# Gate and up projections in Strassen's products in every group from the third on, and two groups ahead of the first down part

## Chip, core and metric

The kernel runs on one core of a Trainium2 chip. The metric is the device time of one execution in microseconds (us). A run gives one such time; beside the runs there is one profiled execution, whose trace gives the start and duration of the instructions on each engine: PE (TensorE, matmuls), PEld (its weight loads), DVE (VectorE), ACT (ScalarE), POOL (GpSimd) and SP (which only issues transfers here).

## What is computed

A decoder trunk of two layers on x of 1 × 512 × 1024 in float32. Each layer has a mixer and then a gated ConvFFN, both behind an RMS norm and with a residual:

```python
def gated_conv_ffn(x, w_gate, w_up, conv_w, conv_b, w_down):
    g = jnp.einsum('bsd,df->bsf', x, w_gate)
    g = causal_dwconv3(g, conv_w) + conv_b
    up = jnp.einsum('bsd,df->bsf', x, w_up)
    return jnp.einsum('bsf,fd->bsd', jax.nn.silu(g) * up, w_down)
...
    hn = rms_norm(h, norm_ffn[layer])
    h = h + gated_conv_ffn(hn, w_gate[layer], w_up[layer], conv_ffn[layer],
                           b_conv_ffn[layer], w_down[layer])
```

The hidden width is 2816, that is 22 tiles of 128 columns. The mixers and the final norm are not touched by the change.

## The kernel before

**Precision.** Every float32 operand is split into a high and a low half of a reduced format (whi/wlo for weights, a_hi/a_lo for activations, hgh/hgl for the normalized input), and a product is three matmuls: high × high, high × low, low × high (`mm3`, lines L133 to L135). A weight is split by ACT (high half, L128) and DVE (low half, L129), or, with `summed`, by ACT twice and an accumulating transfer that POOL issues (L120 to L122); an activation is split by `split` (ACT L247, DVE L249).

**Groups and parts.** The hidden width is worked through in groups of two tiles: group f holds tiles f and f+1, f = 0, 2, ... 20. For each group, gate and up are multiplied, the gate goes through the width-3 convolution (`conv`, ACT L504 and DVE L506) and silu (L512), is multiplied by up, and the result is split into the group's activations a_f and a_f+1. The down projection is done in parts, each over the tiles of one or two groups: in layer 0 `project` (its PSUM tiles are named d; DVE adds them to h at L292), in layer 1 a loop in `ffn1` (PSUM tiles dn; DVE adds to y at L1009). `PARTS` says which tiles each part covers. Each part comes after its groups:

```python
    PARTS = ((0, 2), (2, 6), (6, 10), (10, 14), (14, 18), (18, 22))
    BOTH = (6, 10, 14, 18)
```

so the order before is group 0, down part of tiles 0 and 1, groups 2 and 4, down part of tiles 2 to 5, groups 6 and 8, and so on.

**Four ways to multiply a group** (`hidden`). Group 0 (`direct`, not normalized) multiplies the input as it stands ahead of the norm, 96 matmuls of 512 columns, and the factor of the norm is applied afterwards by DVE (L555) and POOL (L558); while it runs, `normalize` prepares the normalized input (x by DVE at L571, its halves at L575 and L576) and the sums of its blocks (L583 to L586) that the block products need. Group 2 (`direct`, normalized) does the same 96 matmuls on the normalized input. Groups 4, 8, 12, 16 and 20 (`seven`) compute up in Strassen's seven block products and gate as 48 matmuls of 512 columns. Groups 6, 10, 14 and 18 (`both`) compute gate and up each in seven block products. A block product (`multiply`, L623) is 12 matmuls of 256 columns; one seventh less work than the direct form. It needs sums of blocks of the weights, made by DVE into `sum` tiles and split, and the products are put together in `kept` and in the padded rows by ACT copies from PSUM (`both`: L681; `seven`: L765) and DVE adds (`both`: L686). In a group, several products share a PSUM bank (`BANK`): 1, 6, 7 and 4 use bank "a", one after the other.

**Buffers.** Raw weights have 4 buffers, split weights 6 each of high and low, `sum` tiles 3, `kept` 1, activations a 4, convolution tiles c 2, silu tiles s 3, padded rows 3, PSUM 7 banks and one auxiliary. The queues of each engine run in the order that a scheduler writes at build time from the program order and its own estimates; SP issues the loads of raw weights (`fetch`, L110).

Of the kernel before, what the change touches and what calls it, by code (L numbers as in the profile page):

```python
# [8 lines left out]
F32 = mybir.dt.float32  # L9
# [3 lines left out]
ALU = mybir.AluOpType  # L13
PSUM = bass.MemoryType.PSUM

P = 128
# [14 lines left out]
def tile_trunk(ctx: ExitStack, tc: tile.TileContext, x, norm_mix, norm_ffn, final_norm,  # L31
# [3 lines left out]
    nc = tc.nc  # L35
# [9 lines left out]
    def mm_bank(name):  # L45
        return ps_mm.tile([P, 512], F32, tag="mm", name=name)
# [69 lines left out]
    def summed(raw, a, b, name):  # L116

        hi = wp.tile([P, a, b], F32R, tag="whi", bufs=6, name=f"whi_{name}")
        lo = wp.tile([P, a, b], F32R, tag="wlo", bufs=6, name=f"wlo_{name}")
        nc.scalar.activation(lo, raw, AF.Copy, scale=-1.0)  # L120
        nc.gpsimd.dma_start(lo, raw, accum_op=ALU.add)  # L121
        nc.scalar.activation(hi, raw, AF.Copy)  # L122
        return hi, lo

    def parts(raw, a, b, name):
        hi = wp.tile([P, a, b], F32R, tag="whi", bufs=6, name=f"whi_{name}")
        lo = wp.tile([P, a, b], F32R, tag="wlo", bufs=6, name=f"wlo_{name}")
        nc.scalar.activation(hi, raw, AF.Copy)  # L128
        nc.vector.tensor_tensor(lo, raw, hi.bitcast(F32), ALU.subtract)  # L129
        return hi, lo  # L130

    def mm3(ps, lhs, rhs, start, stop):
        nc.tensor.matmul(ps, lhs[0], rhs[0], start=start, stop=False)  # L133
        nc.tensor.matmul(ps, lhs[0], rhs[1], start=False, stop=False)  # L134
        nc.tensor.matmul(ps, lhs[1], rhs[0], start=False, stop=stop)  # L135
# [27 lines left out]
    def hg_k(k):  # L163
        return hg[k][0], hg[k][1]
# [104 lines left out]
    def padded_tile():  # L269
        turn[0] += 1  # L270
        return padded[turn[0] % NPADDED]
# [199 lines left out]
            return nxt  # L471


    PARTS = ((0, 2), (2, 6), (6, 10), (10, 14), (14, 18), (18, 22))
    HALF = S // 2
    BOTH = (6, 10, 14, 18)
    NP = NK // 2
    PAIRS = [k for i in range(NP) for k in (i, i + NP)]

    def ffn_weights(layer, f, order):  # L480
        cs = slice(f * P, (f + 2) * P)
        return {(key, half): fetch(
            (w_ffn_gate if key == "g" else w_ffn_up)[layer][half * 512 : (half + 1) * 512, cs]
            .rearrange("(k p) c -> p k c", p=P), 4, 256, f"{key}{layer}_{f}_{half}")
            for key, half in order}

    class Ffn:
# [143 lines left out]
        def halves(self, hi, lo, src):  # L631
            nc.scalar.activation(hi, src, AF.Copy)
            nc.vector.tensor_tensor(lo, src, hi.bitcast(F32), ALU.subtract)
# [72 lines left out]
            nc.vector.tensor_tensor(s0, kept[:, :2, :], s0, ALU.mult)  # L706
            self.act(f, s[0])

        def seven(self, f):
            layer, ap, n = self.layer, self.ap, f"{self.layer}_{f}"  # L710
            raws = ffn_weights(layer, f, [(key, half) for key in "ug" for half in range(2)])
            r0, r1 = raws["u", 0][0], raws["u", 1][0]
            stat = {}

            def pair(name):
                return self.unit(f"{name}_{n}")

            halves = self.halves

            def put(product, hi_lo, i):  # L720
                stat[product] = hi_lo[0][:, i], hi_lo[1][:, i]

            w = pair("a11")
            halves(w[0][:, 0], w[1][:, 0], r0[:, :, :P])
            put(1, w, 0)
            gate = [parts(*raws["g", 0])]
            s23 = ap.tile([P, 2, 4, P], F32, tag="sum", bufs=3, name=f"s23_{n}")
            s14 = ap.tile([P, 2, 4, P], F32, tag="sum", bufs=3, name=f"s14_{n}")
            nc.vector.tensor_tensor(s14[:, 0], r0[:, :, P:], r1[:, :, P:], ALU.add)
            nc.vector.tensor_tensor(s23[:, 0], s14[:, 0], r0[:, :, :P], ALU.subtract)  # L730
            nc.vector.tensor_tensor(s23[:, 1], r0[:, :, :P], r0[:, :, P:], ALU.subtract)
            w = pair("s23")
            halves(*w, s23)
            put(6, w, 0)
            put(7, w, 1)
            gate.append(parts(*raws["g", 1]))
            nc.vector.tensor_tensor(s14[:, 1], r1[:, :, :P], s23[:, 0], ALU.subtract)
            w = pair("s14")
            halves(*w, s14)
            put(5, w, 0)  # L740
            put(3, w, 1)
            hi, lo = summed(*raws["u", 1])
            for i, product in enumerate((2, 4)):
                c = slice(i * P, (i + 1) * P)
                stat[product] = hi[:, :, c], lo[:, :, c]

            banks = {}

            def multiply(product):
                return self.multiply(banks, f"u{n}", product, stat[product])  # L750

            def gates(half):
                for k in PAIRS[half * 4 : half * 4 + 4]:
                    for j in range(2):
                        if j not in banks:
                            banks[j] = mm_bank(f"g{j}{n}")
                        hi, lo = gate[k // 4]
                        c = slice(j * P, (j + 1) * P)
                        mm3(banks[j], (hi[:, k % 4, c], lo[:, k % 4, c]), hg_k(k),
                            k == PAIRS[0], k == PAIRS[-1])  # L760

            kept = ap.tile([P, 3, HALF], F32, tag="kept", bufs=1, name=f"kept{n}")

            def keep(i, ps):
                nc.scalar.copy(kept[:, i, :], ps)  # L765

            def add(i, ps):
                nc.vector.tensor_tensor(kept[:, i, :], ps, kept[:, i, :], ALU.add)

            keep(0, multiply(1))  # L770
            gates(0)
            keep(1, multiply(6))
            gates(1)
            c, s = [], []
            for j in range(2):
                t = padded_tile()
                nc.scalar.copy(t[:, 2:], banks[j])
                c.append(self.conv(t, f + j))
            keep(2, multiply(7))
            for j in range(2):  # L780
                s.append(self.silu(c[j], f + j))
            ps = multiply(5)
            p2 = multiply(2)
            add(2, ps)
            add(0, p2)
            ps = multiply(4)
            nc.vector.tensor_tensor(s[1][:, HALF:], kept[:, 2, :], s[1][:, HALF:], ALU.mult)
            nc.vector.tensor_tensor(s[1][:, :HALF], ps, s[1][:, :HALF], ALU.mult)
            self.act(f + 1, s[1])
            add(1, multiply(3))  # L790
            s0 = s[0].rearrange("p (a b) -> p a b", a=2)
            nc.vector.tensor_tensor(s0, kept[:, :2, :], s0, ALU.mult)  # L792
            self.act(f, s[0])

        def hidden(self, f, before=lambda i, j: None):
            if f == 0:
                def first(i, j):
                    before(i, j)
                    if (i, j) == (1, 0):
                        self.norm.rstd_tokens()  # L800
                    elif (i, j) == (2, 2):
                        self.r = self.norm.rstd_spread()

                ch = self.pair_weights(0, [("g", 0), ("u", 0), ("g", 1), ("u", 1)])
                rest = self.direct(0, False, (range(4),), ch, first)
                self.ch = self.pair_weights(2, [("g", 0), ("g", 1), ("u", 0), ("u", 1)], "g")
                for kp in range(NP):
                    self.normalize(kp)
                rest()
            elif f == 2:  # L810
                self.direct(2, True, ((0, 1), (2, 3)), self.ch)()
            elif f in BOTH:
                self.both(f)
            else:
                self.seven(f)

    def ffn0(norm):
        nonlocal prm1
        with tc.tile_pool(name="f0", bufs=1) as ap:
            def sums(kp):  # L820
                return [ap.tile([P, 2, HALF], F32R, name=f"t23{i}_{kp}") for i in "hl"]

            ffn = Ffn(0, prm0, norm, ap, sums)
            nxt = None
            for a, b in PARTS:
                for f in range(a, b, 2):
                    ffn.hidden(f)
                if b == NF:
                    prm1 = params1()
                    nxt = Norm("m1", lambda k: prm1("mix", k))  # L830
                project(f"d0_{a}", w_ffn_down[0], ffn.acts, list(range(a, b)), nxt)
            return nxt
# [126 lines left out]
    def ffn1(norm):  # L959
        with tc.tile_pool(name="f1", bufs=1) as ap:  # L960
# [17 lines left out]
                if i < 2:  # L978
                    turn_residual(j, i)

            for a, b in PARTS:
                for f in range(a, b, 2):
                    ffn.hidden(f, before=before)
                last = b == NF
                if last:
# [60 lines left out]
    n = mixer0()  # L1046
    n = ffn0(n)
# [32 lines left out]
```

## Time and profile before

| | |
|---|---|
| runs | 1043.4, 1040.25, 1040.7 us (median 1040.7) |
| profiled execution | 1041.7 us, of which the span (first to last instruction) is 1040.0 us |
| mean granted TensorE clock | 0.983 |
| PE busy | 999.5 us, 96% of the span |
| PEld busy | 865.6 us, 83% |
| DVE busy | 660.4 us, 64% |
| ACT busy | 495.0 us, 48% |
| POOL busy | 91.9 us, 9% |

A row of a group of waits names the engine, tile and line that waited, what released it, and the total, the count and the longest in us. A row of single instructions has its start, its duration, engine, line, operation, written tile and read tiles, then shape, and in brackets the idle time of the engine ahead of it with what ended it. A row of a stretch has the window, its length, the busy time of each engine with its instructions, the granted clock as a share of full speed, the share of the DMA engines' time and GB/s.

### The profile page before, as it was taken

How to read it: one execution, taken by the hardware profiler on the slowest of the kernel's cores; microseconds unless marked ns; L12 is line 12 of the kernel's file. 1: busy time of each engine (PE TensorE's matmuls, PEld its weight loads, DVE VectorE, ACT ScalarE, POOL GpSimd, SP SyncE). 2: the span in 40 equal slices, each digit the busy share in tenths (PEclk: the TensorE clock that was granted, in tenths of full speed). 3: DMA queues.
4: the chain of work that ended last, by engine and by line, in shares of the span. 5: the costliest groups of instructions: out<-in, count | busy, mean ns of one | idle time of the engine just before them, and what ended most of it. 6: DMA issues, size and time to landing. Idle time of an engine off the chain costs nothing.

```text
span 1040.0 us, 13829 instructions
## 1 busy us (share of the span) xinstructions
PE 999.5 (96%) x5475; PEld 865.6 (83%) x5475; DVE 660.4 (64%) x977; ACT 495.0 (48%) x725; POOL 91.9 (9%) x107
## 2 busy tenths in 40 slices
PE   8999996899999999999999999949999999999997
PEld 6888885688988989899888888837889899898985
DVE  5976539638576586756833545495477756767576
ACT  6423447235453536436655434662426436353463
POOL 3041121100000000000300001220000000000000
PEclk9999998799999999999999999979999999999999
DMA  7432244324354453554343223451335544354432
GB/s 234 166 102 81 83 120 110 94 77 123 104 142 112 133 138 106 142 135 124 119 130 101 81 86 97 101 117 45 89 94 142 142 124 141 82 142 142 123 82 81
DMA packets 80462, 119.25 MB, mean 115 GB/s; under 512 B 4133, under 2 KB 53517, under 8 KB 80397
## 3 DMA queue, kind: packets, MB, share of 16 engines
q1 hardware_dynamic: 73580, 98.96, 30.2%
q0 software_dynamic: 5472, 17.83, 9.7%
q10 hardware_dynamic: 1344, 1.58, 0.5%
q8 instruction: 43, 0.70, 0.3%
q14 instruction: 23, 0.18, 0.1%
HBM read 98.42 MB, written 2.10 MB: 97 GB/s over the span
## 4 chain that ended last, share of the span: by engine, by line
PE 91%; DVE 3%; issue 3%; DMA 2%; ACT 0%; SPq 0%; POOL 0%; DVEq 0%; POOLq 0%; ACTq 0%
PE d L133 4%; PE d L134 4%; PE dn L135 4%; PE dn L133 4%; PE dn L134 4%; PE d L135 4%; PE g L133 4%; PE g L134 4%; PE g L135 3%; PE gu L133 2%; PE gu L135 2%; PE gu L134 2%; PE v L133 1%; PE oo L135 1%; PE u L134 1%
## 5 line engine op out<-in xcount | busy, mean ns | idle before, releaser
L133 PE MATMUL dn<-whi_dn,a_hi 128*128 128x512 f32 x176 | 69.3, 395 | 14.9 <-ACT a_hi L247 14.9
L133 PE MATMUL d<-a_hi,whi_d 128*128 128x512 f32 x176 | 68.1, 398 | 14.6 <-ACT a_hi L247 14.6
L134 PE MATMUL d<-a_lo,whi_d 128*128 128x512 f32 x176 | 69.4, 396 | 0.0
L134 PE MATMUL dn<-wlo_dn,a_hi 128*128 128x512 f32 x176 | 68.9, 393 | 0.0
L135 PE MATMUL d<-a_hi,wlo_d 128*128 128x512 f32 x176 | 68.9, 392 | 0.0
L135 PE MATMUL dn<-whi_dn,a_lo 128*128 128x512 f32 x176 | 68.5, 394 | 0.0
L506 DVE SCALAR_TENSOR_TENSOR c<-rows,prm,c 128x512 f32<-128x512 f32 x88 | 66.5, 770 | 0.4
L133 PE MATMUL g<-hgh,whi_g 128*128 128x512 f32 x160 | 62.5, 391 | 0.0
L134 PE MATMUL g<-hgl,whi_g 128*128 128x512 f32 x160 | 62.5, 391 | 0.0
L135 PE MATMUL g<-hgh,wlo_g 128*128 128x512 f32 x160 | 62.2, 389 | 0.0
L1009 DVE TENSOR_TENSOR y<-dn,y 128x512 f32<-128x512 f32 x48 | 32.8, 690 | 37.1 <-PE dn L135 37.0
L133 PEld LDWEIGHTS dn<-whi_dn,a_hi 128*128 128x128 f32 x176 | 33.4, 190 | 22.7 <-ACT a_hi L247 16.0
L133 PEld LDWEIGHTS d<-a_hi,whi_d 128*128 128x128 f32 x176 | 33.3, 191 | 22.6 <-ACT a_hi L247 15.9
L129 DVE TENSOR_TENSOR wlo_dn<-raw_dn,whi_dn 128x1024 fp32r<-128x1024 f32 x22 | 26.8, 1224 | 35.4 <-ACT whi_dn L128 35.4
L129 DVE TENSOR_TENSOR wlo_d<-raw_d,whi_d 128x1024 fp32r<-128x1024 f32 x22 | 26.8, 1224 | 35.4 <-ACT whi_d L128 35.4
L129 DVE TENSOR_TENSOR wlo_g<-raw_g,whi_g 128x1024 fp32r<-128x1024 f32 x24 | 29.3, 1222 | 30.4 <-ACT whi_g L128 26.6
L292 DVE TENSOR_TENSOR h<-d,h 128x512 f32<-128x512 f32 x48 | 32.7, 689 | 20.1 <-PE d L135 19.5
L247 ACT ACTIVATE a_hi<-s 128x512 fp32r<-128x512 f32 x44 | 27.4, 628 | 34.3 <-DVE s L792 13.3
L121 POOL DMA_DIRECT2D wlo_u<-raw_u x18 | 15.4, 858 | 306.6 <-ACT wlo_u L120 175.6
L129 DVE TENSOR_TENSOR wlo_u<-raw_u,whi_u 128x1024 fp32r<-128x1024 f32 x16 | 19.6, 1224 | 34.2 <-ACT whi_u L128 34.1
L135 PEld LDWEIGHTS dn<-whi_dn,a_lo 128*128 128x128 f32 x176 | 33.3, 189 | 8.5 <-DVE a_lo L249 1.3
L134 PEld LDWEIGHTS d<-a_lo,whi_d 128*128 128x128 f32 x176 | 33.6, 191 | 7.9 <-DVE a_lo L249 0.7
(911 smaller groups left out, 3135.7 us busy)
## 6 DMA issues: line engine op xcount, KB each, us to landing
raw_u<-in_w_ffn_up_dram SPq DMA_DIRECT2D x36, 512.0 KB, 3.8
raw_g<-in_w_ffn_gate_dram SPq DMA_DIRECT2D x36, 512.0 KB, 4.5
raw_d<-in_w_ffn_down_dram SPq DMA_DIRECT2D x22, 512.0 KB, 3.6
raw_dn<-in_w_ffn_down_dram SPq DMA_DIRECT2D x22, 512.0 KB, 3.7
wlo_u<-raw_u POOLq DMA_DIRECT2D x18, 512.0 KB, 5.2
wlo_g<-raw_g POOLq DMA_DIRECT2D x12, 512.0 KB, 5.1
raw_oe<-in_w_out_even_dram SPq DMA_DIRECT2D x8, 512.0 KB, 3.5
raw_g<-in_w_ffn_gate_dram SPq DMA_DIRECT2D x16, 256.0 KB, 2.8
```

The costliest lines, as they stand in the source:

```text
L121: nc.gpsimd.dma_start(lo, raw, accum_op=ALU.add)
L129: nc.vector.tensor_tensor(lo, raw, hi.bitcast(F32), ALU.subtract)
L133: nc.tensor.matmul(ps, lhs[0], rhs[0], start=start, stop=False)
L134: nc.tensor.matmul(ps, lhs[0], rhs[1], start=False, stop=False)
L135: nc.tensor.matmul(ps, lhs[1], rhs[0], start=False, stop=stop)
L247: nc.scalar.activation(hi, src, AF.Copy, scale=scale)
L292: nc.vector.tensor_tensor(h[k], ps, h[k], ALU.add)
L506: nc.vector.scalar_tensor_tensor(c, t[:, i : S + i], prm("cf", i * NF + ft), c, op0=ALU.mult, op1=ALU.add)
L1009: nc.vector.tensor_tensor(dst, ps, dst, ALU.add)
```

## The change

`PARTS` gets a first entry that says which groups are multiplied ahead of each part. Groups 0 and 2 now both come ahead of the first down part (tiles 0 and 1); group 4 alone stands ahead of the second, which still covers tiles 2 to 5. Every group from 4 on is multiplied by `both`; `seven` and `BOTH` are gone. For each layer five groups thus change from `seven` to `both`, ten in all.

```diff
-    PARTS = ((0, 2), (2, 6), (6, 10), (10, 14), (14, 18), (18, 22))
+
+    PARTS = (((0, 2), 0, 2), ((4,), 2, 6), ((6, 8), 6, 10), ((10, 12), 10, 14),
+             ((14, 16), 14, 18), ((18, 20), 18, 22))
     HALF = S // 2
-    BOTH = (6, 10, 14, 18)
...
-        def seven(self, f):
...
             elif f == 2:
                 self.direct(2, True, ((0, 1), (2, 3)), self.ch)()
-            elif f in BOTH:
+            else:
                 self.both(f)
-            else:
-                self.seven(f)
...
-            for a, b in PARTS:
-                for f in range(a, b, 2):
+            for groups, a, b in PARTS:
+                for f in groups:
                     ffn.hidden(f)
...
-            for a, b in PARTS:
-                for f in range(a, b, 2):
+            for groups, a, b in PARTS:
+                for f in groups:
                     ffn.hidden(f, before=before)
```

The order of products in `both`, the banks they use and the pairs of groups that a down part covers from tile 6 on are as before. Groups 6 and 8, 10 and 12, 14 and 16, 18 and 20 stand next to each other as before, but now both of each pair are `both`; group 4, which followed group 2, now follows the first down part.

More of the change, by code (lines that the diff above doesn't have):

```diff
@@ L707, in both @@
             self.act(f, s[0])
-        def seven(self, f):
[L710 to L793, printed above, removed]
```

## Prediction

> **What bounds the kernel now.** I read the page first, then the PE waits, then stretches of the span by stage, then the rows of single instructions around the two longest waits.
>
> ```profile
> PE 999.5 (96%) x5475; PEld 865.6 (83%) x5475; DVE 660.4 (64%) x977; ACT 495.0 (48%) x725; POOL 91.9 (9%) x107
> PE 91%; DVE 3%; issue 3%; DMA 2%; ACT 0%; SPq 0%; POOL 0%; DVEq 0%; POOLq 0%; ACTq 0%
> PE dn L133 <- ACT a_hi L247: 14.9, 2, 14.3
> PE d L133 <- ACT a_hi L247: 14.6, 2, 14.2
> ```
>
> TensorE is busy for 999.5 of 1040.0 us and holds 91% of the chain that ended last; VectorE has 64%, ScalarE 48%. So time goes only where PE idles or where PE gets fewer or faster matmuls. Two waits stand out (us in total, times, longest): the first part of each layer's down projection (d in layer 0, dn in layer 1) waits for the activation of group 0. The change touches both sources, the idle and the amount of matmul work.
>
> The stretches, as window, length, then busy time and count of PE, PEld, DVE, ACT, POOL, the granted clock, the DMA share and GB/s:
>
> ```profile
> 172.25:186.71 14.46, 0.26 (x2) 0.00 (x0) 14.46 (x25) 10.74 (x18) 5.33 (x5) 0.62 0.62 125
> 186.71:201.10 14.39, 13.95 (x48) 10.43 (x49) 10.16 (x15) 1.96 (x3) 1.50 (x1) 0.79 0.17 56
> 201.10:222.90 21.80, 21.80 (x98) 18.06 (x97) 8.81 (x10) 7.88 (x11) 0.00 (x0) 1.00 0.15 49
> 265.84:286.00 20.16, 20.16 (x170) 20.16 (x170) 11.24 (x17) 10.73 (x17) 0.86 (x1) 1.00 0.38 105
> 286.00:307.00 21.00, 21.00 (x133) 19.09 (x133) 14.51 (x22) 13.83 (x22) 0.86 (x1) 1.00 0.56 151
> 307.00:328.84 21.84, 21.84 (x98) 18.00 (x98) 16.52 (x26) 6.58 (x8) 0.85 (x1) 1.00 0.47 121
> ...
> 686.92:701.38 14.46, 0.16 (x1) 0.00 (x0) 14.46 (x25) 10.73 (x18) 5.28 (x5) 0.64 0.62 121
> 701.38:715.23 13.85, 13.27 (x48) 9.72 (x49) 9.56 (x13) 1.76 (x3) 1.50 (x1) 0.88 0.08 26
> 780.00:800.30 20.30, 20.30 (x170) 20.18 (x170) 13.26 (x19) 12.26 (x19) 0.85 (x1) 1.00 0.59 157
> 800.30:821.30 21.00, 21.00 (x133) 19.08 (x133) 14.51 (x22) 13.83 (x22) 0.85 (x1) 1.00 0.56 151
> ```
>
> In order: the idle after group 0, the first down part, group 2 (96 matmuls of 512 columns), group 6 (both gate and up in block products), group 8 (only up in block products), a down part; then the same idle and first down part in layer 1, and its groups 6 and 8. Outside the first-part stretches PE has no idle at all.
>
> **First part: two groups ahead of it.** Today PE waits for a_0 and a_1 with DVE busy through all 14.46 us: it normalizes the input of group 2 while it also owes the gating of group 0. Afterwards PE runs on a lowered clock:
>
> ```profile
> 186.71 1.22 PE L133 MATMUL d<-a_hi,whi_d 128*128 128x512 f32 x2 [14.20 <-ACT a_hi L247]
> 188.93 0.63 PE L134 MATMUL d<-a_lo,whi_d 128*128 128x512 f32 x1
> 190.85 1.22 PE L133 MATMUL d<-a_hi,whi_d 128*128 128x512 f32 x2 [0.44 <-ACT a_hi L247]
> 194.30 0.39 PE L133 MATMUL d<-a_hi,whi_d 128*128 128x512 f32 x1
> 705.53 0.50 PE L133 MATMUL dn<-whi_dn,a_hi 128*128 128x512 f32 x1 [0.58 <-ACT a_hi L247]
> ```
>
> At full clock a 512-column matmul costs 21.80 / 96 = 0.227 us, so the 48 of the first part cost 10.9. From the end of group 0 to the end of its down part it takes 14.46 + 14.39 = 28.85 us in layer 0 and 14.46 + 13.85 = 28.31 in layer 1. If group 2 covers the wait completely, 28.85 − 10.9 − 0.26 (the small transpose in the idle stays) = 17.7 and 28.31 − 10.9 = 17.4 us go: together 35.1. Of that 6.4 us are not idle but matmuls on a lowered clock and the second wait (14.39 and 13.85 against 10.9).
>
> The Trainium skill ("TensorE: Matmul & The Clock Gate", the table of what matters for kernels and Part 1) says that an idle gap beyond some 3 us drops the array to half rate and about 3.4 us of activity restore it. That would be a loss of about 1.7 us per restart, an estimate from that page, and a gain of about 32 in place of 35.1; the trace agrees on the direction, but the stretches measure 3.5 and 2.95 us, and I use those.
>
> Is group 2 ready to run at 172.25? It needs the normalized input in pairs (0 and 4, 1 and 5, 2 and 6, 3 and 7), each pair feeding 2 × 6 matmuls = 2.73 us of its gate half, so the last is wanted at 172.25 + 8.2 = 180.4. DVE today:
>
> ```profile
> 172.76 0.70 DVE L576 TENSOR_TENSOR hgl<-x,hgh 128x512 fp32r<-128x512 f32 x1
> 176.96 1.30 DVE L576 TENSOR_TENSOR hgl<-x,hgh 128x512 fp32r<-128x512 f32 x2
> 190.17 0.63 ACT L247 ACTIVATE a_hi<-s 128x512 fp32r<-128x512 f32 x1 [2.76 <-DVE s L561]
> 190.84 0.68 DVE L249 TENSOR_TENSOR a_lo<-s,a_hi 128x512 fp32r<-128x512 f32 x1
> 691.63 1.29 DVE L576 TENSOR_TENSOR hgl<-x,hgh 128x512 fp32r<-128x512 f32 x2
> 704.85 0.63 ACT L247 ACTIVATE a_hi<-s 128x512 fp32r<-128x512 f32 x1 [2.76 <-DVE s L561]
> 182.05 1.50 SPq L110 DMA_DIRECT2D raw_g<-in_w_ffn_gate_dram  x2
> ```
>
> Pair 2/6 is done at 173.46, wanted at 177.7; pair 3/7 at 178.26, wanted at 180.4. In layer 1, 692.92 against 686.92 + 8.2 = 695.1. No wait, with about 2 us in hand. Group 2 then ends at 172.25 + 0.26 + 21.8 = 194.3, and the last operand of group 0 lands at 191.5 today; group 2's own copies and convolutions now stand in the same DVE and ACT queues and push it by an estimated 0.5 us. Cover: 2.3 us; were it gone, each us of lateness costs one us per layer. In layer 1, 686.92 + 21.8 = 708.7 against 705.5, 3.2 us. PSUM has seven banks; group 0 holds four and group 2 opens two at once and two 10.9 us later, by when group 0's two gate banks have been read. Group 4 begins at 205.3 instead of 222.9; its second pair of raw weights is issued at 182.05 and its splits fall into the first down part, where DVE is busy 10 of 14 us and ACT 2. That I cost at nothing; its first products are the ones with the earliest weights.
>
> **Groups 4, 8, 12, 16, 20: gate in block products too.** Each swaps 48 matmuls of 512 columns for 84 of 256. From the rows: 168 matmuls in 20.16 us are 0.120 each; the mixed group is 84 × 0.120 + 48 × 0.227 = 21.0, as measured. Saved per group: 21.00 − 20.16 = 0.84 in layer 0, 21.00 − 20.30 = 0.70 in layer 1, for ten groups 4.2 + 3.5 = 7.7 us.
>
> A rule of the skill speaks against this: "Larger matmuls are more efficient than smaller matmuls, when possible" ("Perfetto Trace Analysis", section on matmuls), and the clock-gate page (back-to-back issue gap) gives 81 ns at 128 columns and 131 at 512 with weight loads in the stream. Interpolated, an estimate from that page, a 256-column one is 0.75 of a 512-column one and the swap would lose 1.9 us per group. The row above disagrees: 0.120 against 0.227 is 0.53. What the row does concede is PEld at 20.16 of 20.16: weight loads have no slack left in such a group.
>
> Added work off PE per group, by code: on DVE four more sums and one more split of 512 columns (as the a_lo row above, 0.68) and three adds from PSUM, 5 × 0.68 + 3 × 0.42 = 4.7 us:
>
> ```profile
> 287.28 0.42 DVE L686 TENSOR_TENSOR kept<-u_6e,kept 128x256 f32<-128x256 f32 x1
> ```
>
> On ACT the splits come to some 2.5 wide copies more, 2.6 us by the wlo_u row below (1.05), and POOL issues one more summed weight. A part of two groups and a down part becomes 2 × 20.2 + 21.8 = 62.2 us of PE against 11.24 + 14.51 + 16.52 + 4.7 = 47 us of DVE. Throughput holds; order decides.
>
> **Two such groups in a row** (8 pairs: 6-8, 10-12, 14-16, 18-20 in each layer) are new, and no row shows them. Today ACT behind group 6:
>
> ```profile
> 285.47 0.71 ACT L504 ACTIVATE c<-rows,prm 128x512 f32<-128x512 f32 x1
> 286.08 0.71 ACT L512 ACTIVATE s<-c,prm 128x512 f32<-128x512 f32 x1
> ...
> 288.59 0.71 ACT L512 ACTIVATE s<-c,prm 128x512 f32<-128x512 f32 x1
> 289.20 0.61 ACT L247 ACTIVATE a_hi<-s 128x512 fp32r<-128x512 f32 x1
> 289.73 1.05 ACT L120 ACTIVATE wlo_u<-raw_u 128x1024 fp32r<-128x1024 f32 x1
> 291.45 0.63 ACT L247 ACTIVATE a_hi<-s 128x512 fp32r<-128x512 f32 x1 [0.68 <-DVE s L706]
> 291.99 0.35 ACT L765 COPY kept<-u_8a 128x256 f32<-128x256 f32 x1
> ...
> wlo_u<-raw_u POOLq DMA_DIRECT2D x18, 512.0 KB, 5.2
> ```
>
> The convolution, silu and split of the old group keep ACT until 291.99, 6.0 us after the new group began, and only then is its first product copied out of PSUM. Today that copy is needed at 7 us (12 block matmuls and 24 wide ones come first: 1.44 + 5.47). In the changed kernel the gate's product 6 follows in the same bank and, in program order, would start after three products, at 4.3 us. The built order moves other products ahead of it, 55 matmuls in all, so it starts at 55 × 0.120 = 6.6. My queue of ACT work puts the copy's end at 6.4 to 6.7, more splits standing ahead of it than today. Two more near ties: the second summed weight of up, issued near 6.5 and 5.2 us under way, lands at 11.7 where it is wanted at 11.5 to 11.9; and the down part after the pair wants a_8 at 24 × 0.227 = 5.4 us, where the tail above gives 291.45 + 0.63 − 286.00 = 6.1 for the same operand with other splits in its way, about 5 without them. Bounds for each pair: nothing, if the ties fall well; 2.4 us (6.7 − 4.3), if the reordering buys nothing; less than nothing is excluded, since PE's matmul count is fixed. I take 0.5, because the nearest row with such a group on a full engine queue (layer 1, 20.30 against 20.16) lost 0.14, and there are three ties: 8 × 0.5 = 4 us.
>
> **Sum.** −35.1 − 7.7 + 4.0 = −38.8 us. The profiled execution took 1041.7, so 1002.9; it lies 1.0 above the median of 1040.7, so the forecast is 1002. With no stall and both layers at 0.84 it would be 1040.7 − 35.1 − 8.4 = 997. A difference of 0.3% (3 us, the spread of the three runs) is what a measurement here can tell from none.
>
> **Rivals.**
> 1. *The pairs stall.* ACT's backlog delays the first copy by the full 2.4 us in every pair. Eight pairs lose 19 instead of 4: 1017. For: ACT's rows above are back to back. Against: the built order was made around that wait.
> 2. *The idle moves.* Group 2 or group 4 runs into unfinished normalization, late a_1 or late splits, 5 us per layer: 1012. For: DVE is busy in every microsecond of the old idle, and the cover is only 2 us. Against: the rows already have all normalized pairs before they would be wanted.
> 3. *Slower.* DVE and ACT fall behind for good inside each pair: each of the copies and PSUM adds waits behind the splits of the next part, banks stay held, and raw weight buffers come free late. It decides once a pair loses more than (35.1 + 7.7) / 8 = 5.4 us; at 6 us each, 48 − 42.8 = +5, 1046. Against: 47 us of DVE in 62.
> 4. *Weight loads bind.* PEld is at 100% in such groups; if each product cost 3.4 us more per group (0.75 of a wide matmul, 0.170 × 168 − 0.170 × 84 − 48 × 0.227 = 3.4), ten groups add 34 and the result is about 1040.7 − 35.1 + 34 + 4 = 1044. The skill's figures above point there, both measured stretches against it.
>
> That the change does nothing can't be: the built order has group 2 ahead of the first down matmul in both layers and 84 products in all ten groups.
>
> **Chances.** Forecast, 994 to 1010: 0.73. Rival 1: 0.12. Rival 2: 0.09. Rival 3: 0.04. Rival 4: 0.01; another 0.01 for no change. The range 995 to 1014 takes the forecast case, rival 2 and some of rival 1. Faster 0.94, same 0.01, slower 0.05.
>
> **What would show it.** Right: no PE wait on a_hi L247 above 1 us; the granted clock at 1.00 after group 0 and 0.99 or more overall; PE's count 5475 + 10 × 36 = 5835, its busy time near 986 (999.5 − 7.7 − the 5.4 that the first parts' matmuls are busy beyond 10.9); group 4 starting about 17.5 us earlier; 20.2 us for groups 4 to 20. Wrong: PE waits on ACT copies (L681) or DVE adds (L686) of some 2 us, eight times; a wait on hgl or on summed weights at the head of group 2 or 4; stretches of block products above 21 us.

## The result and the profile after

The changed kernel took 1006.16 us (median of four runs, 1005.03 to 1007.18) against 1041.34 (four runs, 1040.25 to 1043.4): a ratio of 0.966, 95% interval 0.9639 to 0.9681, or 35 us less. Its profiled execution took 1007.18 us, with a span of 1005.5 and a mean granted clock of 0.996.

The page and PE's waits of the changed kernel (engine, tile and line that waited, what released it, total, times, longest):

```profile
PE 988.0 (98%) x5835; PEld 875.6 (87%) x5835; DVE 699.3 (70%) x1057; ACT 521.9 (52%) x775; POOL 100.8 (10%) x117
PE 81%; issue 7%; DMA 5%; DVE 5%; ACT 2%; POOL 0%; SPq 0%; ACTq 0%; DVEq 0%; POOLq 0%
PE g_18e L624 <- DVE rows L692: 3.0, 2, 2.4
PE xt_ps L357 <- DMA xt<-in_x_dram: 2.4, 1, 2.4
PE g_6e L624 <- DVE rows L692: 1.1, 1, 1.1
PE u_10a L624 <- ACT kept L682: 1.0, 1, 1.0
PE g_10e L624 <- DVE rows L692: 0.3, 1, 0.3
```

Both 14 us waits on a_hi are gone. PE has 360 matmuls more, as counted, and is busy 11.5 us less. New are five small waits in groups of block products: four on DVE's add to the gate's rows (L692, L691 before) and one on an ACT copy. DMA has come up from 2% to 5% of the chain that ended last, DVE from 3% to 5%, issue from 3% to 7%.

The stretches of the changed kernel, columns as before: group 2 and then the first down part in layer 0, group 4, group 8; group 18 in layer 0; and in layer 1 groups 6, 8, 18 (a down part stands between 8 and the next).

```profile
173.58:195.35 21.77, 21.77 (x98) 18.02 (x96) 21.77 (x35) 16.70 (x27) 6.82 (x6) 1.00 0.47 97
195.35:206.23 10.88, 10.88 (x50) 9.01 (x49) 10.88 (x17) 5.68 (x7) 0.88 (x1) 1.00 0.46 112
206.23:226.38 20.15, 20.15 (x170) 20.15 (x168) 11.82 (x17) 11.40 (x19) 0.86 (x1) 1.00 0.56 153
268.35:288.58 20.23, 20.23 (x171) 20.23 (x169) 14.75 (x23) 14.39 (x24) 0.86 (x1) 1.00 0.59 158
434.89:455.88 20.99, 20.40 (x170) 20.20 (x168) 14.34 (x23) 12.13 (x19) 1.72 (x2) 1.00 0.43 114
742.67:764.32 21.65, 20.58 (x170) 20.25 (x168) 15.41 (x24) 13.70 (x21) 1.86 (x3) 1.00 0.63 155
764.32:784.48 20.16, 20.16 (x171) 20.16 (x169) 14.03 (x21) 13.75 (x23) 0.86 (x1) 1.00 0.61 154
932.80:955.82 23.02, 20.58 (x169) 20.25 (x168) 14.81 (x23) 13.22 (x21) 1.87 (x3) 1.00 0.62 137
```

The first down part takes 10.88 us at clock 1.00, with DVE just as busy as in the old idle: its work now lies under PE's. Groups that were mixed are at 20.15 to 20.24. But group 18 of layer 1 takes 23.02 us where PE is busy 20.58, and groups 6 and 10 there take 21.65 and 22.10: the prediction had named stretches of block products above 21 us as a sign that it was wrong.

The account, from the start of one stage's first matmul to that of the next. From the wide matmuls of group 0 to the end of group 2 and the first down part: 65.69 us before and 47.72 after in layer 0 (157.17 to 222.86, 158.51 to 206.23), 65.14 and 47.71 in layer 1: −35.4. The ten groups that changed form: −4.0 and −4.2. The eight groups that had that form already: +0.8 and +5.9. The start, ahead of the first block and not touched by the change, took 1.3 us more (PE's wait for the first input alone 2.4 us against 1.0), and about +1.0 came in other places: −34.5, the difference of the two profiled executions.

### The profile page after: what moved, and what is told of

Same layout as the page of the kernel before. It is cut to its first block, busy times and chain, and to the rows that moved or that the text cites. A ratio compares the mean times of both kernels' runs of the same rounds, so it can differ in the third digit from the quotient of the medians.

```text
span 1005.5 us, 14738 instructions
## 1 busy us (share of the span) xinstructions
PE 988.0 (98%) x5835; PEld 875.6 (87%) x5835; DVE 699.3 (70%) x1057; ACT 521.9 (52%) x775; POOL 100.8 (10%) x117
## 4 chain that ended last, share of the span: by engine, by line
PE 81%; issue 7%; DMA 5%; DVE 5%; ACT 2%; POOL 0%; SPq 0%; ACTq 0%; DVEq 0%; POOLq 0%
PE gu L133 3%; PE gu L134 3%; PE gu L135 3%; PE d L133 3%; PE d L134 3%; PE d L135 3%; PE dn L133 2%; PE dn L135 2%; PE dn L134 2%; DMA raw_g<-in_w_ffn_gate_dram 2%; PE u L135 1%; PE oo L135 1%; PE u L134 1%; PE oo L133 1%; PE u L133 1%
## 5 line engine op out<-in xcount | busy, mean ns | idle before, releaser
L121 POOL DMA_DIRECT2D wlo_g<-raw_g x22 | 19.1, 868 | 382.1 <-ACT wlo_g L120 315.9
L120 ACT ACTIVATE wlo_g<-raw_g 128x1024 fp32r<-128x1024 f32 x22 | 23.2, 1055 | 42.4 <-PE dn L134 42.4
L513 ACT ACTIVATE s<-c,prm 128x512 f32<-128x512 f32 x44 | 30.8, 716 | 21.5 <-DVE c L507 21.5
L633 ACT ACTIVATE whi_s12u<-s12u 128x1024 fp32r<-128x1024 f32 x18 | 18.9, 1049 | 43.2 <-PE d L134 33.8
L633 ACT ACTIVATE whi_s12g<-s12g 128x1024 fp32r<-128x1024 f32 x18 | 19.1, 1061 | 41.7 <-DVE s12g L654 36.1
L135 PEld LDWEIGHTS d<-a_hi,wlo_d 128*128 128x128 f32 x176 | 33.0, 188 | 6.8
```

The lines of the kernel that those rows point to most:

```text
L513: nc.scalar.activation(s, c, AF.Silu, bias=self.prm("bf", ft))
```

## Experiment 1: each half of the change alone

`e1_order_only` is the kernel before with the new `PARTS` and its two loops; `e2_both_only` is the changed kernel with the old order:

```diff
-    PARTS = (((0, 2), 0, 2), ((4,), 2, 6), ((6, 8), 6, 10), ((10, 12), 10, 14),
+    PARTS = (((0,), 0, 2), ((2, 4), 2, 6), ((6, 8), 6, 10), ((10, 12), 10, 14),
```

> The kernel before with only the new order (groups 0 and 2 ahead of the first down part); groups 4, 8, 12, 16, 20 keep gate as wide matmuls. If the two halves of the change are independent and the order alone brings what the stretches of the changed kernel show (18.0 us in layer 0, 17.4 in layer 1), the time is 1041.3 - 35.4 = 1006, as fast as the whole change. If the order needed the block products of group 4 to be covered, PE waits ahead of group 4 and it is above 1010.

> The changed kernel with the old order (group 0, first down part, groups 2 and 4); block products for gate and up in all groups from 4 on. By the changed kernel's stretches the five swapped groups of each layer save 4.0 and 4.2 us and the first group of each pair loses 0.8 in layer 0 and 5.9 in layer 1: 1041.3 - 1.4 = 1040, no change that can be told. By the prediction's own sum (7.7 saved, 4.0 lost) it is 1037.6. PE waits on the DVE adds of the gate's bank e in layer 1 (groups 6, 10, 14, 18) should be seen with the old order too, 5 to 7 us in all.

Measured: the order alone 1007.21 us, ratio 0.9654 (0.9639 to 0.9669); the block products alone 1041.58 against 1042.43, ratio 0.9988 (0.9976 to 1.0). The first equals the whole change. The second is no change that can be told, as the account of the stretches has it; the prediction's own sum of −3.7 us (1038.7 beside this 1042.43) lies just outside the interval's 1040 to 1042.4.

The order alone, its two first down parts; then PE's waits with the block products alone:

```profile
194.21:205.09 10.88, 10.88 (x50) 9.01 (x48) 10.88 (x17) 4.87 (x7) 0.00 (x0) 1.00 0.23 81
691.64:702.52 10.88, 10.88 (x49) 9.01 (x48) 10.88 (x17) 4.26 (x6) 0.00 (x0) 1.00 0.25 75
```

```profile
PE dn L133 <- ACT a_hi L247: 14.6, 2, 13.3
PE d L133 <- ACT a_hi L247: 14.0, 2, 13.2
PE g_18e L624 <- DVE rows L692: 2.2, 1, 2.2
PE g_6e L624 <- DVE rows L692: 1.2, 1, 1.2
PE u_10a L624 <- ACT kept L682: 1.1, 1, 1.1
PE g_14e L624 <- DVE rows L692: 0.4, 1, 0.4
```

Group 4 needs no block products to be ready for the order to pay. The small waits come with the block products under either order: layer 1's groups 6, 10, 14 and 18 take 21.72, 22.14, 20.96 and 24.27 us here, and 20.31 each with the order alone.

## Experiment 2: is the slow first down part a matter of the clock?

The prediction booked 6.4 us in the two first parts to "matmuls on a lowered clock and the second wait". `e3_keep_warm` keeps TensorE busy through the idle:

```diff
+        def keep_warm(self):
+            ps = aux_bank(f"warm{self.layer}")
+            for i in range(58):
+                nc.tensor.matmul(ps, hg[1][0][:, :P], hg[0][0], start=i == 0, stop=i == 57)
...
                     ffn.hidden(f)
+                    if f == 0:
+                        ffn.keep_warm()
```

> The kernel before with 58 wide matmuls on data at hand (13.2 us, result unused) put into PE's idle ahead of each layer's first down part, so that TensorE stays busy; nothing else is moved. If the slow matmuls after the idle (14.39 and 13.85 us for work of 10.9) are a matter of the clock alone, the first parts take about 10.9 and 6.4 us go. If the second operand a_1, ready only at 190.8 and 705.5, sets their start, PE waits for it instead (about 2 us more of wait per layer) and only what lies behind it speeds up, 10.25 to 8.9 and 9.7 to 9.3: 1 to 2 us in all.

One execution: 1038.29 us, the kernel before beside it 1042.43. Its two first parts:

```profile
187.25:199.27 12.02, 11.36 (x49) 9.04 (x49) 9.90 (x15) 1.96 (x3) 1.52 (x1) 1.00 0.16 52
699.66:711.70 12.04, 11.38 (x49) 8.96 (x49) 9.33 (x13) 1.77 (x3) 1.52 (x1) 1.00 0.08 28
```

The granted clock is 1.00 where it was 0.79 and 0.88, and the parts take 12.02 and 12.04 us where they took 14.39 and 13.85. So 2.4 + 1.8 = 4.2 us of the 6.4 were the clock. About 1.1 us in each layer stays, 0.66 of it PE's wait for a_1. My expectation of 1 to 2 us in all was wrong, for a_1 holds PE up by 0.66 us and not by 2:

```profile
191.41 1.19 PE L133 MATMUL d<-a_hi,whi_d 128*128 128x512 f32 x4 [0.66 <-ACT a_hi L247]
703.83 0.50 PE L133 MATMUL dn<-whi_dn,a_hi 128*128 128x512 f32 x1 [0.65 <-ACT a_hi L247]
```

In the kernel before, the clock was halved over the first 5.95 us of the part in layer 0 and the first 3.28 us in layer 1:

```profile
186.71:192.66 5.95, 5.51 (x11) 3.48 (x12) 4.81 (x7) 1.33 (x2) 1.50 (x1) 0.50 0.14 48
701.38:704.66 3.28, 3.28 (x7) 1.99 (x7) 3.28 (x4) 0.70 (x1) 1.50 (x1) 0.50 0.30 106
```

The clock's part is larger than the 1.7 us per restart that I had estimated from the Trainium skill ("TensorE: Matmul & The Clock Gate", Part 1), in layer 0 by 0.7 us; in layer 1 it agrees.

## Experiment 3: what costs the first group of a pair

The prediction had put its stalls into the second group of each pair, where ACT works off the first one's tail. The trace shows that place as forecast and nearly free. ACT in the changed kernel, behind the start of group 8 at 268.35, and PE's product 6 in bank a:

```profile
273.57 1.05 ACT L120 ACTIVATE wlo_u<-raw_u 128x1024 fp32r<-128x1024 f32 x1
274.53 0.35 ACT L682 COPY rows<-g_8a 128x256 f32<-128x256 f32 x1
```

```profile
269.67 0.28 PE L624 MATMUL g_8a<-hgh,wlo_a 128*128 128x256 f32 x1
274.99 0.33 PE L624 MATMUL g_8a<-t23h,whi_s12g 128*128 128x256 f32 x1
```

The copy ends 6.53 us into the group (forecast 6.4 to 6.7) and product 6 starts at 6.64, behind the 55 matmuls that the built order puts ahead of it; the group loses 0.08 us. The loss is in the first group. Follow the longest, group 18 in layer 1 (from 932.80), through ACT, POOL, SP, DVE and PE of the changed kernel:

```profile
930.73 1.06 ACT L120 ACTIVATE wlo_g<-raw_g 128x1024 fp32r<-128x1024 f32 x1 [10.60 <-PE dn L134]
932.09 0.86 POOL L121 DMA_DIRECT2D wlo_g<-raw_g  x1 [33.96 <-ACT wlo_g L120]
936.82 0.86 POOL L121 DMA_DIRECT2D wlo_u<-raw_u  x1 [3.87 <-DMA wlo_g<-raw_g]
936.69 0.37 SPq L110 DMA_DIRECT2D raw_g<-in_w_ffn_gate_dram  x1
944.27 0.37 SPq L110 DMA_DIRECT2D raw_u<-in_w_ffn_up_dram  x1
949.19 0.69 DVE L653 TENSOR_TENSOR s12u<-raw_u,raw_u 128x512 f32<-128x512 f32 x1 [4.20 <-DMA raw_u<-in_w_ffn_up_dram]
950.93 0.42 DVE L692 TENSOR_TENSOR rows<-g_18e,rows 128x256 f32<-128x256 f32 x1
951.41 0.39 PE L624 MATMUL g_18e<-hgh,whi_s34g 128*128 128x256 f32 x1 [2.44 <-DVE rows L692]
```

ACT can start the summed weight of group 18 only when the down part frees split-weight buffers (10.60 us of wait). The accumulating transfers then hold two of the four raw buffers, and only as these come free does SP load the second halves of group 20: gate at 936.69, up at 944.27. DVE has the sums of group 20 ahead of group 18's add in its queue, idles 4.20 us until that weight lands, and only then does the add that frees bank e for product 3. When group 20 was a mixed group, its gate halves were needed by ACT and DVE for a split alone and its up halves were loaded first: in the kernel before, the last of them is issued 11 us ahead of group 18 (958.41, the group starts at 969.26), and DVE makes its sums from 972.45 on without a wait.

Two readings are possible: the weight comes late for lack of a raw buffer, or DVE and ACT have too much to do in that group. Three variants tell them apart, with the changed kernel beside them. `e4_fifth_raw` gives the second up half of groups 6, 10, 14 and 18 a raw buffer of its own (and takes one of three silu tiles for the room; the tiles yf of the last norm share that tag and have two as well):

```diff
+            raw = extra.tile([P, a, b], F32, tag="raw5", bufs=1, name=f"raw_{name}")
...
+            extra if (key, half) == ("u", 1) and f % 4 == 2 else None)
...
-            s = self.ap.tile([P, S], F32, tag="s", bufs=3, name=f"s{self.layer}_{ft}")
+            s = self.ap.tile([P, S], F32, tag="s", bufs=2, name=f"s{self.layer}_{ft}")
```

`e5_u_split` and `e6_no_summed` replace the accumulating transfer, the first for up, the second for both:

```diff
-                hi, lo = summed(*raws[key, 1])
+                hi, lo = (summed if key == "g" else parts)(*raws[key, 1])
```

```diff
-                hi, lo = summed(*raws[key, 1])
+                hi, lo = parts(*raws[key, 1])
```

> The changed kernel again, as the measure for the variants beside it: 1006, with waits of PE on DVE's add to the gate's rows (L692) in the first group of a pair, above all in layer 1 (groups 6, 10, 14, 18 at 21.7, 22.1, 20.4 and 23.0 us where 20.16 is free of stalls).

> The changed kernel with a fifth buffer for raw weights: the second up half of the first group of each pair gets its own, so the raw weights of the second group no longer wait until that group's summed transfers have let go (paid with two silu tiles in place of three). If the stall is DVE standing in its queue ahead of a weight that lands late, because the load waits for a raw buffer, groups 6, 10, 14 and 18 of layer 1 come to about 20.3 us and 6 us go: 1000. If it is DVE and ACT having too much work in the first group, it stays at 1006.

> The changed kernel with up's second half split by ACT and DVE and not by ACT and an accumulating transfer: the raw buffer is free after about 1.2 us of DVE and not after a transfer of 5 to 7 us, and DVE has 18 x 1.2 = 22 us more work. Late buffer: the raw weights land some 5 us earlier, the stalls of layer 1 go, 1000 to 1002. Too much work on DVE: the stalls grow, above 1006.

> As the kernel before this one, and gate's second half too: no accumulating transfer in any group from 4 on, 44 us more DVE work. Late buffer: no stall left in the first groups, 1000 or a little above, unless the split weights of the down part hold it up. Too much work on DVE: clearly above 1006, more than the kernel with only up changed.

| kernel | us (median) | ratio to before, 95% | groups 6, 10, 14, 18 of layer 1, us |
|---|---|---|---|
| changed kernel again | 1006.58 | 0.9662 (0.9646 to 0.9678) | 21.14, 22.00, 20.60, 24.29 |
| fifth raw buffer | 1002.09 | 0.9616 (0.9601 to 0.963) | 20.32, 20.95, 20.32, 20.33 |
| up split, not summed | 999.99 | 0.9596 (0.9581 to 0.961) | 20.15, 20.16, 20.15, 20.15 |
| none summed | 999.16 | 0.9587 (0.9572 to 0.9602) | 20.16, 20.16, 20.16, 20.16 |

Group 18 of layer 1 in these four, in that order:

```profile
930.38:954.67 24.29, 21.80 (x170) 21.48 (x169) 15.50 (x24) 13.81 (x21) 1.86 (x3) 0.93 0.63 148
```

```profile
929.13:949.46 20.33, 20.33 (x170) 20.21 (x169) 14.70 (x22) 12.95 (x20) 1.87 (x3) 1.00 0.56 134
```

```profile
928.38:948.53 20.15, 20.15 (x169) 20.15 (x168) 15.64 (x23) 12.00 (x19) 1.00 (x2) 1.00 0.48 135
```

```profile
928.03:948.19 20.16, 20.16 (x170) 20.15 (x169) 17.44 (x26) 11.36 (x19) 0.00 (x0) 1.00 0.39 112
```

DVE has the most work in the last of these, where PE has no stall (17.44 us against 15.50), so too much work isn't it. The extra buffer, with no work taken away or added, brings 4.5 us, and freeing the raw weights earlier 6.6 and 7.4. With the extra buffer POOL issues the summed weight of group 18 just as far ahead of the group as without it, 0.7 us (928.41 and 932.09), so the wait for split-weight buffers is not what changed. But SP loads group 20's second up half 3.9 us into the group and not 11.5, and DVE's wait for it is 1.30 us and not 4.20:

```profile
937.26 0.69 DVE L657 TENSOR_TENSOR s12u<-raw_u,raw_u 128x512 f32<-128x512 f32 x1 [1.30 <-DMA raw_u<-in_w_ffn_up_dram]
```

In the last kernel SP loads the two halves 0.5 and 4.5 us into the group, not 3.9 and 11.5, and DVE waits 0.34 us:

```profile
928.54 0.37 SPq L110 DMA_DIRECT2D raw_g<-in_w_ffn_gate_dram  x1
932.54 0.37 SPq L110 DMA_DIRECT2D raw_u<-in_w_ffn_up_dram  x1
937.01 0.69 DVE L653 TENSOR_TENSOR s12u<-raw_u,raw_u 128x512 f32<-128x512 f32 x1 [0.34 <-DMA raw_u<-in_w_ffn_up_dram]
940.29 0.42 DVE L692 TENSOR_TENSOR rows<-g_18e,rows 128x256 f32<-128x256 f32 x1
```

The late buffer is shown. With the fifth buffer the four groups of the table lose 6.1 us less, what was expected, though group 10 still loses 0.8. The whole gains less, 4.5: the stretch from the last down part's start to the end takes 30.7 us (969.69 to 1000.4) against 29.5 without the buffer (974.83 to 1004.3). The yf tiles, down from three to two, are used there, but giving them up wasn't tried apart.

Not all of group 18's 24.29 us is the wait itself. In that execution PE stalls for 2.49 us and the granted clock then falls to about half; in the first execution of the same kernel, behind a stall of 2.44 us, it stays at 1.00, and the group takes 23.02. The stretch behind the stall, first with 24.29 and then with 23.02 us:

```profile
949.00:952.00 3.00, 2.98 (x14) 2.98 (x15) 2.45 (x6) 0.72 (x1) 0.86 (x1) 0.52 0.57 109
951.41:955.82 4.41, 4.41 (x36) 4.41 (x37) 4.28 (x9) 2.36 (x4) 0.86 (x1) 1.00 0.76 119
```

Why group 18 stalls longer than 6, 10 and 14 stays open. `e6_no_summed` beats both kernels: 42.5 us below the kernel before and 7.4 below the changed one. The order alone was 35.2 below its kernel before, so in this form the block products bring 7.3 us, near the 7.7 that the prediction had booked for them without stalls.

## Why the prediction held

It said 1002 (995 to 1014); measured 1006.16.

- **First part.** Forecast −17.7 and −17.4, measured −18.0 and −17.4, and −35.2 for the order alone. The cover held, and for the reason given: PE waits for neither hgl nor a_hi in group 2 or in a down part; the last operand of group 0 is ready 1.9 us ahead of the down part in each layer (a_lo ends at 193.46, the part starts at 195.35; 687.93 and 689.81), where the prediction had 2.3 and 3.2. Splitting the 35 us into idle and clock was not needed for the sum; the keep-warm run puts the clock's share at 4.2 us.
- **Fewer matmuls.** Forecast −4.2 and −3.5, measured −4.0 and −4.2. Seven block products are one eighth less work than the direct form, not one seventh as the text ahead of the prediction has it: 84 × 256 columns against 48 × 512, or 1.36 of 10.9 us. But a matmul of 256 columns takes 0.120 us, more than half of 0.227, and 84 of them give 0.55 us back; 0.8 is left. So the rows bear out the rule of the Trainium skill that larger matmuls are more efficient ("Perfetto Trace Analysis", section on matmuls), by 6% for a column; it is too little to undo the smaller count.
- **Two groups in a row.** This is the step that failed: "I take 0.5 … 8 × 0.5 = 4 us", in the second group of a pair. There 0.08 us was lost in layer 0 and nothing in layer 1; the first groups lost 0.8 + 5.9 = 6.8 (0.84 and 5.94). That 4 and 6.8 are of one size is luck: they are different stalls, in different groups. So the block products brought 8.2 − 6.8 = 1.4 us here, and not 7.7 − 4.0 = 3.7; that the time still came near the forecast is owed to the first part. I had looked for DVE and ACT being busy and had costed throughput; what bound was DVE standing idle in its queue behind a late weight. Its "Throughput holds; order decides" did stand: 38 us more DVE work in the last kernel (737.4 busy against 699.3) cost nothing.
- **The rest.** Between the profiled executions the change is −34.5 where the sum had −38.8. Of these 4.3 us, 2.8 are that term; the start, 1.3 us longer in this execution, is not part of the change.
- **Rivals.** The idle did not move; the stalls of 2.4 us in every pair did not come, though one of 2.44 came once by another way; no backlog built up, though raw-weight buffers that come free late, a part of rival 3, are what cost the first groups their time; and weight loads, busy throughout such a group, did not make it longer than the 20.15 us of the rows before.

## What to carry to other kernels

When PE waits for the tail of one group, put the next group's matmuls ahead of the consumer; check its operands and the banks against the old rows. Here the whole idle went. When a group's form is swapped for one with fewer matmuls, look not only at what its own engines have to do but at what its prefetch puts into their queues during the group before: an engine that works through its queue in order, as DVE did here, holds up the small adds that PE needs while it waits for a weight. Work moved onto an engine with time to spare can be worth it if it lets a buffer go sooner.

## What the runs showed of the hardware

After 14 us of idle the first down part took 2.4 and 1.8 us more than with TensorE kept busy, and the granted clock was 0.50 for its first 5.95 and 3.28 us. In group 18 of layer 1 a stall of 2.49 us was followed by 0.52 over 3 us, one of 2.21 us (`e2_both_only`) by 0.50 over 3.3 us, and one of 2.44 us (the changed kernel's first execution) by 1.00; what decides between them is not shown. A transfer that accumulates 512 KB took 4.5 us from issue to landing where it ran alone (issued 932.09; the next load into its buffer is issued at 936.69) and 7.3 us where a load of 512 KB ran beside it (issued 936.82; next load 944.27).
